# Building the Mixer's cosine and sine tables in one pass over split partitions

## The chip, the cores and the metric

The kernel runs on one core of a Trainium2 chip. It uses five engines, each with an instruction stream of its own that it executes in order: TensorE (PE: matmuls, and PEld: its weight loads), VectorE (DVE), ScalarE (ACT), GpSimd (POOL) and SyncE (SP, which here issues the DMA transfers). The metric is the device time of one execution in microseconds (us), as the median of several runs.

## The reference

One decoder layer with 1024 tokens of width 1024, in float32: a first SwiGLU feed-forward block, a mixer (half of its channels a short gated convolution, half an S5 state-space model, "SSM"), and a second feed-forward block. Each is modulated by `cond` (adaLN). What matters here:

```python
def reference(x, cond, ...):
    c_act = jax.nn.silu(cond)
    mod = c_act @ w_mod[l] + b_mod[l]        # shifts, scales and gates
    h = modulate(rms_norm(x, ffn1_norm[l]), sh1, sc1)
    x = x + 0.5 * g1 * swiglu(h, ffn1_w_gate[l], ffn1_w_up[l], ffn1_w_down[l])
    h = modulate(rms_norm(x, mix_norm[l]), sh2, sc2)
    b_gate, c_gate, v, u = jnp.split(h @ w_in[l], ...)
    y_conv = short_conv_mixer(b_gate, c_gate, v, conv_w[l])
    y_ssm = s5_mixer(u, lambda_re[l], lambda_im[l], log_dt[l], ...)
    ...                                       # norms, w_out, second feed-forward block

def s5_mixer(u, lambda_re, lambda_im, log_dt, b_re, b_im, c_re, c_im, ...):
    lam = lax.complex(lambda_re, lambda_im)
    dt = jnp.exp(log_dt)[:, None]
    lam_bar = jnp.exp(lam * dt)               # 32 groups x 64 states
    b_bar = ((lam_bar - 1) / lam)[..., None] * b
    bu = jnp.einsum('gpc,bsgc->bsgp', b_bar, uf)
    # state_t = lam_bar * state_(t-1) + bu_t, for all 1024 tokens
    _, states = lax.associative_scan(_ssm_combine, (a, bu), axis=1)
    y = jnp.einsum('gcp,bsgp->bsgc', c, states).real + d_skip * uf
    ...
```

The state-space model needs powers of `lam_bar`. The kernel keeps their phase as a rotation: for each group a table of cosines and one of sines over 128 steps.

## The kernel before

Every float32 product is made from high and low halves: `mm3` issues three matmuls of 128x512. The feed-forward blocks multiply by a seven-product scheme. `seven` makes one of the groups fa4 to fa10 of the first block in two sides, g and then u, each with seven left blocks of 4 `mm3`, that is 12 matmuls each. VectorE adds the products up out of PSUM banks. The seventh left block (S4) uses bank C again, so it waits until the side's third add has read that bank:

```python
SEVEN = (("A11", "A"), ("S1", "C"), ("S2", "B"), ("S3", "D"), ("A12", "A"), ("A22", "E"), ("S4", "C"))
...
elif n == 3:
    u3 = t2k(nm + "u3")
    add(u3, u2, "D")
    add(t1, u3, "C")      # the third add: fa5gt<-fa5gu,fa5gC in the trace
    out(1, 1, t1)
```

Tiles are named after the group and the side: `fa5gu`, `fa5gt` are partial sums of group fa5's gate side, `fa5gC` is its bank C, `fa5uu`, `fa5ut` are the same for the up side. At the end of a u side VectorE also makes some twenty operations that keep the result and its sums (`fa5A`, `fa5S`), stored to `kept...` for the down stages, where they come back as `fa1lA`, `fa1lS` and so on. The down stage of the first four groups, `down7("fad0")`, multiplies these by the weights `in_ds` and adds the products onto `x`. Every weight goes from a `raw` buffer through ScalarE (`CAST w<-raw`, the high half) and VectorE (`w<-raw,w`, the low half); GpSimd makes the sums of weight blocks (`sums`, lines 164, 165, 173 and 175 in `combine` and `split_done`).

Work that is not the feed-forward block's, the preparation of the Mixer above all, is put between the matmuls by a planner. `Clock` counts one tick for each `mm3`, and after every `period` ticks it takes one step of the side queue, that is, runs its generator up to the next `yield`. The period is 4 ticks in fa1 to fa3 and 7.75 in fa4 to fa10. The side queue holds `side1`: `ssm_base` (base tables for all groups), some combinations, and `ssm_batch(b)` for eight batches of four groups. `gate1` adds the steps of the modulation tiles (`wm`) while there are any. When group fa10 begins, what is left of the queue is run to its end, the side pools are closed, and `x` is loaded again into the space (`load_x`, first half at once, second half during `fad0`).

`ssm_batch` makes for each batch, with the names of the trace: `bb` and `cl`, `bl` (input and output coefficients, with `clt`, `blt` beside them), the rotors, and from two small TensorE products `kc` (with its diagonal `dg`) and `mi`. The tag `bt` has four buffers, which `cl`, `clt`, `bl`, `blt`, `rot`, `rott`, `kc`, `dg` and `mi` take in turn, so a tile waits until the one before in its buffer is read out. All results go to DRAM (`co_d`, `si_d`, `mk_d`, `mi_d`, `mo_d`) and come back in the Mixer stage. The rotors of before take two passes of 128 partitions: `rotors(0, subtract)` makes the cosines and `rotors(1, add)` the sines, with the second half of the partitions a repetition of the first, with the sine's sign turned there because `ro[1][hi]` has been negated. `st` are the step tables (`rs` in the trace), `bs` the base tables (`rt`).

Nearly all instructions are issued through the wrapper `InOrder`, whose `call` is line 107, so they carry L107 in the profile and are told apart by their tiles. The functions that the change touches:

Of the kernel before, what the change touches and what calls it, by code (L numbers as in the profile page):

```python
# [16 lines left out]
AF = mybir.ActivationFunctionType  # L17
ALU = mybir.AluOpType
# [213 lines left out]
def hymba_layer(ctx: ExitStack, tc, x_d, wm1_d, wmod_d, gu1_d, gs1_d, ds1_d, wl1_d, win_d, wout_d, glu_d, gu2_d, gs2_d, wd2_d, ds2_d, wl2_d, cols_d, cond_d, lam_d, bc_d, out_d):  # L232
    nc = tc.nc
    V, A, T, SP = (InOrder(tc, e) for e in (nc.vector, nc.scalar, nc.tensor, nc.sync))
# [30 lines left out]
    def sm(shape, name):  # L265
        return sm_ps.tile(shape, F32, tag="sm", name=name)
# [75 lines left out]
    def parts(name, where="A"):  # L342
        t = mov(name, where)
        return t[:, 0, :], t[:, 1, :]
# [427 lines left out]
    st = sm([P, 8], "p_st")  # L772
# [30 lines left out]
    for k in range(KT):  # L803
# [7 lines left out]
        for h in range(2):  # L811
            hi, lo = parts(f"h1{k}_{h}")
# [41 lines left out]
    co_d = scratch.tile([NB, P, GB * P], F32, name="co_d")  # L854
    si_d = scratch.tile([NB, P, GB * P], F32, name="si_d")
# [28 lines left out]
    def ssm_base(sb1):  # L884
# [4 lines left out]
        def s32(name):  # L889
            return sb1.tile([P, G], F32, tag=name, name=name)[:]  # L890
# [20 lines left out]
        dt, ar, th, r = s32("dt"), s32("ar"), s32("th"), s32("rr")  # L911
# [10 lines left out]
        ro = [s32("ro_r"), s32("ro_i")]  # L922
# [49 lines left out]
        lo, hi = slice(0, 64), slice(64, 128)  # L972
# [10 lines left out]
        V.tensor_tensor(out=w[0], in0=r, in1=r, op=ALU.mult)  # L983
        V.tensor_tensor(out=w[0], in0=w[0], in1=w[0], op=ALU.mult)
        V.tensor_tensor(out=r8[:], in0=w[0], in1=w[0], op=ALU.mult)
        V.tensor_scalar(out=ro[1][hi], in0=ro[1][hi], scalar1=-1.0, scalar2=None, op0=ALU.mult)
        cur = (ro[0], ro[1])
        base = [sb1.tile([P, 16, G], F32, tag=f"rb{i}", name=f"rb{i}") for i in range(2)]
        baset = [sb.tile([P, G, 16], F32, tag=f"rt{i}", name=f"rt{i}") for i in range(2)]
# [15 lines left out]
        for tab, cnt in ((base, 16), (step, 8)):  # L1005
# [3 lines left out]
            while n < cnt:  # L1009
# [4 lines left out]
                doubled(f"c{cnt}_{n}")  # L1014
                yield
                n *= 2
        for i in range(2):
            A.copy(baset[i][:], base[i][:].rearrange("p i g -> p g i"))
        yield
        zero = sb1.tile([CH, 112], F32, name="zero")  # L1020
        V.memset(zero[:], 0.0)
# [9 lines left out]
    def ssm_batch(b):  # L1031
# [9 lines left out]
        def bt(name):  # L1041
            return bp.tile([P, 576], F32, tag="bt", name=name, bufs=4)
# [20 lines left out]
        def v3(a):  # L1063
            return a[:, :512].rearrange("p (g m i) -> p g m i", g=GB, m=8)

        bs = [a[:, gs, :].unsqueeze(2).to_broadcast([P, GB, 8, 16]) for a in ssm["base"]]
        st = [a[:, :, gs].rearrange("p m g -> p g m").unsqueeze(3).to_broadcast([P, GB, 8, 16]) for a in ssm["step"]]

        def rotors(i, op):
            r, t = bt(f"rot{b}_{i}"), bt(f"rott{b}_{i}")  # L1070
            V.tensor_tensor(out=v3(r), in0=st[0], in1=bs[i], op=ALU.mult)
            V.tensor_tensor(out=v3(t), in0=st[1], in1=bs[1 - i], op=ALU.mult)
            yield
            V.tensor_tensor(out=r[:, :512], in0=r[:, :512], in1=t[:, :512], op=op)
            SP.dma_start((co_d, si_d)[i][b], r[:, :512])

        yield from rotors(0, ALU.subtract)
        yield

        kp = sm([CH, 512], f"kp{b}")  # L1080
# [5 lines left out]
        for g in range(GB):  # L1086
            T.transpose(tp[:, g * P : (g + 1) * P], bl[:, g * P : (g + 1) * P], ident[:])
        yield from gate1()
        yield from rotors(1, ALU.add)
        yield from gate1()  # L1090
        kc = bt(f"kc{b}")
        kc3 = kc[:CH, :512].rearrange("p (g m) -> p g m", g=GB)
# [4 lines left out]
            out=dg3,  # L1097
            in0=ident[:CH, :CH].unsqueeze(1).to_broadcast([CH, GB, CH]),
            in1=ssm["lam"][:CH, 3, gs].unsqueeze(2).to_broadcast([CH, GB, CH]),
            op=ALU.mult,  # L1100
# [11 lines left out]
    def gate1():  # L1112

        if fetched:
            mod_tile(mod_home if later[0][0] == G1 else None)
            yield
# [4 lines left out]
    def side1():  # L1121
        with tc.tile_pool(name="sb1", bufs=1, side="right") as sb1:
            yield from ssm_base(sb1)
        bps.append(side_open.enter_context(tc.tile_pool(name="bp", bufs=1, side="right")))
        mod_home.pool = side_open.enter_context(tc.tile_pool(name="wmp", bufs=1, side="right"))
        for _ in range(2):
            mod_fetch(mod_home)
        yield from combos(act1, "h1", "BBB")
        for b in range(NB):
            yield from ssm_batch(b)  # L1130
# [530 lines left out]
```

## Time and profile before

| quantity | value |
|---|---|
| runs | 1750.65, 1750.65 and 1752.18 us, median 1750.65 |
| profiled execution, its span | 1750.3 us |
| mean granted TensorE clock | 0.989 |
| VectorE instructions | 2286, busy 1300.6 us (74%) |
| ScalarE instructions | 934, busy 566.0 us (32%) |
| DMA moved | 304.54 MB, mean 174 GB/s |

The profile describes one execution. A row of a group gives line, engine, operation, output and inputs, shape and count, then busy time and mean duration in ns, then the engine's idle time ahead of these instructions and what ended it. Rows of the timeline give the start and the duration in us, and in brackets the idle time ahead with its releaser. Rows of the waits give what waited for what, us in total, times and longest. The row of a DMA issue gives SyncE's time for issuing; the landing is a separate row.

The span in 40 slices shows where VectorE is nearly full (each digit is the busy share of a slice in tenths):

```profile
PE   4999999999999999999999899989999999999996
DVE  7999999999855687744656977967777666676656
```

The tables of the Mixer are built in the first quarter, beside the groups fa1 to fa9; the down stage `fad0` lies at 480 to about 590 us.

### The profile page before, as it was taken

How to read it: one execution, taken by the hardware profiler on the slowest of the kernel's cores; microseconds unless marked ns; L12 is line 12 of the kernel's file. 1: busy time of each engine (PE TensorE's matmuls, PEld its weight loads, DVE VectorE, ACT ScalarE, POOL GpSimd, SP SyncE). 2: the span in 40 equal slices, each digit the busy share in tenths (PEclk: the TensorE clock that was granted, in tenths of full speed). 3: DMA queues.
4: the chain of work that ended last, by engine and by line, in shares of the span. 5: the costliest groups of instructions: out<-in, count | busy, mean ns of one | idle time of the engine just before them, and what ended most of it. 6: DMA issues, size and time to landing. Idle time of an engine off the chain costs nothing.

```text
span 1750.3 us, 20808 instructions
## 1 busy us (share of the span) xinstructions
PE 1677.9 (96%) x7532; PEld 1379.6 (79%) x7532; DVE 1300.6 (74%) x2286; ACT 566.0 (32%) x934; POOL 351.1 (20%) x241
## 2 busy tenths in 40 slices
PE   4999999999999999999999899989999999999996
PEld 3788887878787888887877778778888888888886
DVE  7999999999855687744656977967777666676656
ACT  4223234444322221332113424423343443322221
POOL 0000132222222221100000022023323322333211
PEclk9999999999999999999999999999999999999998
DMA  8245544444597877134654450113444334669312
GB/s 319 85 145 196 207 167 165 182 169 178 196 391 266 326 256 292 56 84 149 210 157 140 144 191 25 48 46 135 157 162 173 147 133 156 239 242 366 115 49 96
DMA packets 101080, 304.54 MB, mean 174 GB/s; under 512 B 19057, under 2 KB 34673, under 8 KB 89842
## 3 DMA queue, kind: packets, MB, share of 16 engines
q1 hardware_dynamic: 100978, 303.22, 48.4%
q8 instruction: 59, 0.97, 0.2%
q14 instruction: 43, 0.35, 0.1%
HBM read 212.47 MB, written 86.51 MB: 171 GB/s over the span
## 4 chain that ended last, share of the span: by engine, by line
PE 76%; DVE 14%; DMA 5%; issue 2%; POOL 1%; ACT 1%; SPq 1%; DVEq 0%; POOLq 0%; ACTq 0%
PE wo L107 4%; PE fald L107 3%; DVE w L107 3%; PE p L107 2%; PE fb10d L107 2%; PE fbd_0B L107 2%; PE fbd_1B L107 2%; PE u L107 2%; DMA swz<-si 2%; PE b L107 1%; DVE x L107 1%; PE c L107 1%; PE fa3u L107 1%; PE fb0g L107 1%; PE fa2g L107 1%
## 5 line engine op out<-in xcount | busy, mean ns | idle before, releaser
L107 ACT CAST w<-raw 128x512 fp32r<-128x512 f32 (+1 forms) x358 | 236.2, 689 | 484.3 <-issue 75.0
L107 DVE TENSOR_TENSOR w<-raw,w 128x512 fp32r<-128x512 f32 (+1 forms) x358 | 295.9, 845 | 107.3 <-ACT w L107 106.5
L164 POOL TENSOR_TENSOR sums<-raw 128x512 f32<-128x512 f32 x50 | 71.4, 1429 | 451.5 <-DMA raw<-in_gs 263.3
L173 POOL TENSOR_TENSOR raw<-sums,raw 128x512 f32<-128x512 f32 x50 | 77.7, 1554 | 371.1 <-DVE w L107 358.9
L175 POOL TENSOR_TENSOR raw<-raw 128x512 f32<-128x512 f32 x50 | 77.5, 1549 | 89.6 <-DVE w L107 73.0
L107 DVE CUSTOM_DVE_ANT_0 wm<-wm,cact 128x1024 f32<-128x1024 f32 x56 | 76.6, 1375 | 16.9 <-DMA wm<-in_wmod 16.9
L165 POOL TENSOR_TENSOR raw<-raw 128x512 f32<-128x512 f32 x50 | 77.3, 1547 | 3.2
L366 POOL TENSOR_TENSOR n3aq<-n3aq,n3aq 128x512 f32<-128x512 f32 x5 | 8.3, 1666 | 281.4 <-DMA wm<-in_wmod 255.7
L107 PE MATMUL p<-h,w 128*128 128x512 f32 x192 | 50.0, 423 | 8.0 <-DVE h L107 5.1
L107 DVE TENSOR_TENSOR w<-sums,w 128x512 fp32r<-128x512 f32 x50 | 52.5, 1063 | 3.6 <-ACT w L107 3.0
L107 PEld LDWEIGHTS p<-h,w 128*128 128x128 f32 x192 | 39.4, 207 | 18.4 <-DVE h L107 6.4
L107 PE MATMUL v<-h,w 128*128 128x512 f32 x192 | 46.9, 395 | 0.0
L107 PE MATMUL c<-h,w 128*128 128x512 f32 x192 | 46.6, 395 | 0.0
L107 PE MATMUL wo<-oa,w 128*128 128x512 f32 x192 | 45.6, 392 | 0.9 <-DVE w L107 0.7
L107 PE MATMUL b<-h,w 128*128 128x512 f32 x192 | 45.6, 394 | 0.0
L107 PE MATMUL wo<-ob,w 128*128 128x512 f32 x192 | 45.5, 392 | 0.0
L107 PE MATMUL u<-h,w 128*128 128x512 f32 x192 | 44.7, 392 | 0.2 <-DVE h L107 0.2
L107 PEld LDWEIGHTS wo<-oa,w 128*128 128x128 f32 x192 | 35.8, 188 | 9.0 <-DVE w L107 1.1
L107 PEld LDWEIGHTS u<-h,w 128*128 128x128 f32 x192 | 35.7, 188 | 8.2 <-DVE h L107 0.6
L107 PEld LDWEIGHTS wo<-ob,w 128*128 128x128 f32 x192 | 35.8, 188 | 7.7 <-DVE ob L107 0.4
L107 PEld LDWEIGHTS b<-h,w 128*128 128x128 f32 x192 | 35.6, 188 | 7.1
L107 PEld LDWEIGHTS c<-h,w 128*128 128x128 f32 x192 | 35.4, 188 | 7.0
(1565 smaller groups left out, 4056.2 us busy)
## 6 DMA issues: line engine op xcount, KB each, us to landing
raw<-in_gs SPq DMA_DIRECT2D x34, 1024.0 KB, 5.5
wm<-in_wmod SPq DMA_DIRECT2D x56, 512.0 KB, 5.3
raw<-in_ds SPq DMA_DIRECT2D x16, 1024.0 KB, 7.2
raw<-in_gu SPq DMA_DIRECT2D x10, 1024.0 KB, 7.0
mw<-in_wm SPq DMA_DIRECT2D x8, 1024.0 KB, 12.8
x<-in_x SPq DMA_DIRECT2D x16, 512.0 KB, 8.0
raw<-in_win SPq DMA_DIRECT2D x8, 1024.0 KB, 5.4
raw<-in_wl SPq DMA_DIRECT2D x5, 1024.0 KB, 6.7
```

What stands on the lines that cost most here:

```text
L107: r = getattr(self.engine, name)(*args, **kw)
L164: self.G.tensor_tensor(out=f, in0=r[2], in1=r[1], op=ALU.subtract)
L165: self.G.tensor_tensor(out=r[1], in0=r[1], in1=r[0], op=ALU.subtract)
L173: self.G.tensor_tensor(out=r, in0=s["t3"], in1=r, op=ALU.add)
L175: self.G.tensor_tensor(out=r, in0=self.chunk(j, 3), in1=r, op=ALU.subtract)
L366: nc.gpsimd.tensor_tensor(out=a, in0=a, in1=sq[:, :n], op=ALU.add)
```

## The change

The two passes become one. The cosines are made on partitions 0 to 63 and the sines on 64 to 127: the base tables `baset` are laid out for that, half by half, with the sign of one of them turned by ScalarE (so the negation of `ro[1][hi]` is dropped), and one product, one more product and one add on 128 partitions give both tables. ScalarE then negates the sines into `rott`'s upper half. Where before one store each filled `co_d[b]` and `si_d[b]`, four stores of 64 partitions now fill the two halves of each: the cosines twice, the sines, and the negated sines. The two tables in DRAM are the same as before. One `rotors` call less means three VectorE instructions less per batch (24 in all), one `yield` less per batch, eight more ScalarE instructions for the negations and two more for `baset`, and 32 instead of 16 stores.

```diff
-        V.tensor_scalar(out=ro[1][hi], in0=ro[1][hi], scalar1=-1.0, scalar2=None, op0=ALU.mult)
...
-        for i in range(2):
-            A.copy(baset[i][:], base[i][:].rearrange("p i g -> p g i"))
+        turned = [b[:].rearrange("p i g -> p g i") for b in base]
+        A.copy(baset[0][lo], turned[0][lo])
+        A.copy(baset[0][hi], turned[1][hi])
+        A.activation(baset[1][lo], turned[1][lo], AF.Copy, scale=-1.0)
+        A.copy(baset[1][hi], turned[0][hi])
         yield
...
-        def rotors(i, op):
-            r, t = bt(f"rot{b}_{i}"), bt(f"rott{b}_{i}")
-            V.tensor_tensor(out=v3(r), in0=st[0], in1=bs[i], op=ALU.mult)
-            V.tensor_tensor(out=v3(t), in0=st[1], in1=bs[1 - i], op=ALU.mult)
+        def rotors():
+
+            r, t = bt(f"rot{b}"), bt(f"rott{b}")
+            V.tensor_tensor(out=v3(r), in0=st[0], in1=bs[0], op=ALU.mult)
+            V.tensor_tensor(out=v3(t), in0=st[1], in1=bs[1], op=ALU.mult)
             yield
-            V.tensor_tensor(out=r[:, :512], in0=r[:, :512], in1=t[:, :512], op=op)
-            SP.dma_start((co_d, si_d)[i][b], r[:, :512])
-
-        yield from rotors(0, ALU.subtract)
+            V.tensor_tensor(out=r[:, :512], in0=r[:, :512], in1=t[:, :512], op=ALU.add)
+            A.activation(t[64:128, :512], r[64:128, :512], AF.Copy, scale=-1.0)
+            for half in (slice(0, 64), slice(64, 128)):
+                SP.dma_start(co_d[b, half], r[0:64, :512])
+            SP.dma_start(si_d[b, 0:64], r[64:128, :512])
+            SP.dma_start(si_d[b, 64:128], t[64:128, :512])
+
+        yield from rotors()
         yield
...
         yield from gate1()
-        yield from rotors(1, ALU.add)
         yield from gate1()
```

The order of the instructions on the engines is set by a scheduler, so other instructions move too. VectorE ahead of the third add of fa5's u side (`fa5ut<-fa5uu,fa5uC`), in the kernel before; `w` are halves of weights, `rot_0` and `rot_1` the first and second pass:

```order
640 L107 TENSOR_TENSOR rot_0_2891<-rs_989,rt_987 128x512
641 L107 TENSOR_TENSOR bl_2828<-bl_2828,blt_2829 128x512
642 L107 TENSOR_TENSOR rott_0_2892<-rs_990,rt_988 128x512
643 L107 TENSOR_TENSOR rot_0_2891<-rot_0_2891,rott_0_2892 128x512
644 L107 TENSOR_TENSOR fa5uu_2741<-fa5ut_2688,fa5uB 128x512
645 L107 TENSOR_TENSOR w_2746<-raw_2568,w_2746 128x512 x2
646 L107 TENSOR_TENSOR rot_1_2980<-rs_989,rt_988 128x512
647 L107 TENSOR_TENSOR rott_1_2981<-rs_990,rt_987 128x512
648 L107 TENSOR_TENSOR fa5uu_2782<-fa5uu_2741,fa5uD 128x512
649 L107 TENSOR_TENSOR rot_1_2980<-rot_1_2980,rott_1_2981 128x512
650 L107 TENSOR_TENSOR fa5ut_2688<-fa5uu_2782,fa5uC 128x512
```

The same place in the changed kernel:

```order
629 L107 TENSOR_TENSOR blt_2712<-tab_932,bb_2660 128x512
630 L107 TENSOR_TENSOR bl_2711<-bl_2711,blt_2712 128x512
631 L107 TENSOR_TENSOR rot_2747<-rs_988,rt_986 128x512
632 L107 TENSOR_TENSOR rott_2748<-rs_989,rt_987 128x512
633 L107 TENSOR_TENSOR rot_2747<-rot_2747,rott_2748 128x512
634 L107 TENSOR_TENSOR w_2726<-raw_2381,w_2726 128x512 x2
635 L107 TENSOR_TENSOR fa5uu_2764<-fa5ut_2724,fa5uB 128x512
636 L107 TENSOR_TENSOR w_2769<-raw_2584,w_2769 128x512 x2
637 L107 TENSOR_TENSOR fa5uu_2794<-fa5uu_2764,fa5uD 128x512
638 L107 TENSOR_TENSOR fa5ut_2724<-fa5uu_2794,fa5uC 128x512
```

Between the side's first add (`fa5uu` from bank B) and its third, three rotor instructions stood before, and none stands there now.

VectorE in the changed kernel, behind the rotors of the batch that falls into group fa6's g side; `dg` and `kc` take the buffers that `rott` and `rot` leave:

```order
681 L107 TENSOR_TENSOR rot_3019<-rs_988,rt_986 128x512
682 L107 TENSOR_TENSOR rott_3020<-rs_989,rt_987 128x512
683 L107 TENSOR_TENSOR rot_3019<-rot_3019,rott_3020 128x512
684 L107 TENSOR_TENSOR fa6gu_2999<-fa6gu_2999,fa6gE 128x512
685 L107 TENSOR_TENSOR w_3043<-sums_2954,w_3043 128x512
686 L107 TENSOR_TENSOR w_3043<-raw_2731,w_3043 128x512
687 L107 TENSOR_TENSOR fa6gu_2984<-fa6gu_2984,fa6gC 128x512
688 L107 TENSOR_TENSOR w_3083<-raw_2731,w_3083 128x512 x2
689 L107 TENSOR_TENSOR dg_3112<-ident,lam 16x64
690 L107 TENSOR_TENSOR bb_3163<-prm_3160,qr 128x64
691 L107 TENSOR_TENSOR kc_3110<-kc_3110,dg_3112 16x4x16
```

In the kernel before, `rot_1` of this batch (made in fa6's u side) has `dg` behind it only after the kept sums of fa6:

```order
704 L107 TENSOR_TENSOR rott_1_3289<-rs_990,rt_987 128x512
705 L107 TENSOR_TENSOR fa6ut_3054<-fa6uu_3136,fa6uC 128x512
706 L107 TENSOR_TENSOR rot_1_3288<-rot_1_3288,rott_1_3289 128x512
707 L107 TENSOR_TENSOR fa6ut_3054<-fa6ut_3054,fa6gt_2895 128x512
708 L107 TENSOR_TENSOR fa6gc_2987<-fa6gc_2987,fa6uA 128x512
...
727 L107 TENSOR_TENSOR w_3263<-raw_3061,w_3263 128x512
728 L107 TENSOR_TENSOR dg_3330<-ident,lam 16x64
```

`dg` has moved from 22 rows behind the last rotor add to 6 rows behind it.

SyncE ahead of the weights `in_ds` that the first down stage waits for, in the kernel before; `x` is the reload, 512 KB:

```order
268 L107 DMA fa3lS_4638<-kept3S_559 128x1024
269 L107 DMA fa4lS_4640<-kept4S_566 128x1024
270 L107 DMA x_1_4306<-in_x 128x1024
271 L107 DMA raw_4780<-in_ds 128x2048
272 L107 DMA raw_4812<-in_ds 128x2048
```

In the changed kernel the eight reloads stand together some forty rows earlier, ahead of the last `in_gs` load, and none is left in front of `in_ds`:

```order
238 L107 DMA x_1_4289<-in_x 128x1024
239 L107 DMA x_1_4291<-in_x 128x1024
240 L107 DMA raw_4152<-in_gs 128x2048
...
277 L107 DMA fa3lS_4623<-kept3S_559 128x1024
278 L107 DMA fa4lS_4625<-kept4S_566 128x1024
279 L107 DMA raw_4765<-in_ds 128x2048
280 L107 DMA raw_4797<-in_ds 128x2048
```

The loads have moved past the stores of fa9's and fa10's kept tiles, and the `in_ds` loads follow the `kept` loads directly.

## The prediction

> **What bounds the kernel now.** I read the busy shares first, then what TensorE waits for, and then the stages in which it waits.
>
> ```profile
> PE 1677.9 (96%) x7532; PEld 1379.6 (79%) x7532; DVE 1300.6 (74%) x2286; ACT 566.0 (32%) x934; POOL 351.1 (20%) x241
> ```
>
> TensorE is busy for 1677.9 of the profiled 1750.3 us, so this is a matmul kernel with small holes. The change adds no matmul and takes none away; it can only act through those holes. The waits of TensorE (what it waited for: us in total, times, longest) from 180 to 480 us, the stage in which the tables are built, and from 480 to 700:
>
> ```profile
> PE fa5uC L107 <- DVE fa5ut L107: 2.1, 1, 2.1
> PE fa7gC L107 <- DVE fa7gt L107: 2.6, 1, 2.6
> PE fa9gC L107 <- DVE fa9gt L107: 1.2, 1, 1.2
> ...
> PE fad_0A L107 <- DVE w L107: 2.8, 2, 1.7
> PE fad_0B L107 <- ACT w L107: 1.8, 1, 1.8
> ```
>
> The first three are one mechanism. The last left block of a side (S4) goes into bank C, which is free only when VectorE has made the side's third add (`fa?gt` or `fa?ut` from bank C). VectorE is late there, because the Mixer's tables stand in the same in-order queue. In the table by stretch (length, busy us and matmuls of PE, then PEld, DVE, ACT, POOL, clock, DMA share, GB/s) the price of each hole is seen by its missing matmuls:
>
> ```profile
> 290.00:310.00 20.00, 17.90 (x80) 14.52 (x79) 19.90 (x27) 6.78 (x12) 6.58 (x4) 1.00 0.39 159
> 350.00:370.00 20.00, 17.43 (x71) 13.90 (x70) 19.30 (x33) 8.72 (x17) 6.81 (x4) 0.91 0.53 183
> 430.00:450.00 20.00, 18.79 (x83) 15.25 (x82) 19.97 (x27) 7.66 (x14) 5.94 (x4) 1.00 0.59 212
> 530.00:550.00 20.00, 17.98 (x72) 14.11 (x71) 11.93 (x17) 2.56 (x5) 4.67 (x4) 0.92 0.96 369
> 550.00:570.00 20.00, 18.16 (x70) 13.95 (x69) 10.82 (x14) 5.14 (x10) 7.00 (x5) 0.91 0.53 189
> 570.00:590.00 20.00, 20.00 (x90) 16.58 (x89) 11.56 (x16) 2.90 (x5) 5.38 (x4) 1.00 0.88 348
> ```
>
> A full stretch holds 90 matmuls, 0.222 us each. The table stage misses 10, 19 and 7 of them: 2.2 + 4.2 + 1.6 = 8.0 us for 5.9 us of waits. The down stage `fad0` misses 18 and 20: 8.4 us. These 16.4 us are all that the change can win near its place. VectorE is nearly full in the first three stretches (19.3 to 19.97 of 20) and little over half full in the others.
>
> **The part on VectorE.** What the rotors take now (first three rows, 160 to 470 us, mean ns of one and idle time ahead), and what one takes undisturbed (min/median/max):
>
> ```profile
> L107 DVE TENSOR_TENSOR rot<-rot,rott 128x512 f32<-128x512 f32 x16 | 16.0, 1001 | 0.2
> L107 DVE TENSOR_TENSOR rott<-rs,rt 128x512 f32<-128x512 f32 x16 | 15.3, 959 | 2.1 <-DMA co_d<-rot 2.1
> L107 DVE TENSOR_TENSOR rot<-rs,rt 128x512 f32<-128x512 f32 x16 | 14.2, 885 | 0.1
> ...
> L107 DVE TENSOR_TENSOR rot<-rs,rt x16: 676/690/1784, 169.4 to 451.5; 128x512 f32<-128x512 f32 x16
> ```
>
> Together 45.5 us; half of them goes, 24 instructions and 22.7 us. At 0.60 us (the spacing of undisturbed neighbours, as 359.18 and 359.78 below) it is 14.4. The small negation of `ro[1]`, one instruction of under 0.4 us, goes too.
>
> That is not 22.7 us of the end, because the work is also pressed together. Each batch loses a `yield`: five steps instead of six once the modulation tiles are through. A step falls due every 7.75 ticks of three matmuls, 7.75 × 3 × 0.222 = 5.2 us. Eight batches so end about 41 us earlier, where now the last store of a table is issued at
>
> ```profile
> 463.15 0.53 SPq L107 DMA_DIRECT2D mi_d<-mi  x1
> ```
>
> The table work per batch, from the spacings in this piece of VectorE's timeline ahead of the dearest hole (start, duration), with TensorE's row last:
>
> ```profile
> 353.20 0.20 DVE L107 TENSOR_TENSOR dg<-ident,lam 16x64 f32<-16x64 f32 x1
> 353.42 0.69 DVE L107 TENSOR_TENSOR fa6S<-fa6uu,fa6S 128x512 fp32r<-128x512 f32 x1
> 354.03 1.32 DVE L107 TENSOR_TENSOR kc<-kc,dg 16x64 f32<-16x64 f32 x1
> 355.28 0.20 DVE L107 TENSOR_TENSOR bb<-prm,qr 128x64 f32<-128x64 f32 x1
> ...
> 358.50 0.76 DVE L107 TENSOR_TENSOR cl<-cl,clt 128x576 f32<-128x576 f32 x1
> 359.18 0.68 DVE L107 TENSOR_TENSOR fa7gu<-fa7gu,fa7gD 128x512 f32<-128x512 f32 x1
> 359.78 0.68 DVE L107 TENSOR_TENSOR w<-raw,w 128x512 fp32r<-128x512 f32 x1
> 360.38 0.68 DVE L107 TENSOR_TENSOR fa7gt<-fa7gu,fa7gC 128x512 f32<-128x512 f32 x1
> ...
> 361.21 4.24 PE L107 MATMUL fa7gC<-h1S,w 128*128 128x512 f32 x12 [2.57 <-DVE fa7gt L107]
> ```
>
> `dg` and `kc` take 0.2 + 1.25, `bb` and `cl` 3.9 less one add of the side among the rows left out (0.6), `bl` three times 0.60, the rotors six times 0.60: 10.2 us in six steps, 1.7 us a step. Afterwards 8.4 us in five steps, again 1.7. So the load per 5.2 us hardly changes; what ends is its duration. I counted what of it stands between two third adds in the two orders, at these spacings. From a u side to the next g side VectorE also makes the kept sums, and before, little fits: with 4.7, 4.7 and 5.3 us (fa6 to fa7, fa7 to fa8, fa8 to fa9) two of three boundaries made a hole, and so did the 9.5 us from fa5's g to its u. Afterwards the heavy ones are 5.3 us (fa5 to fa6), 4.7 (fa7 to fa8) and, from g to u, 7.1 (fa6) and 7.7 (fa7); behind fa8's u side there is none. Fitting the holes of before gives some 6.3 us of room from g to u, 2.3 from u to g, and a carried lead of at most 3.3. By that the new order waits 5.0 us instead of 5.9: the holes at fa5u and fa9g go, others come in fa6 to fa8. At 8.0 us lost for 5.9 waited, that is 6.8 lost, **1.2 won**.
>
> The dearest hole shows more than its wait: 2.57 us idle, but 19 matmuls (4.2 us) gone at a granted clock of 0.91, where the hole of 2.1 us lost 2.2 at 1.00. The Trainium skill ("TensorE: Matmul & The Clock Gate", "HAM oscillation — how this bites in real kernels") says that only idle gaps over about 3.4 us cost clock; by it the win would be 5.9 − 5.0 = 0.9. The trace disagrees at 2.57 us, so I keep 1.2.
>
> **ScalarE and the stores.** Eight negations of 64x512 are added, and the two turned copies of `rt` become four; the rows nearest to them, and the landing of the stores of before:
>
> ```profile
> L107 ACT COPY mi<-tp 128x512 f32<-128x512 f32 x8 | 4.6, 575 | 0.0
> L107 ACT COPY rt<-rb x2: 1147/1149/1151, 118.4 to 119.5; 128x512 f32<-128x512 f32 x2
> ...
> L107 SPq DMA_DIRECT2D co_d<-rot x8: 320/326/727, 177.6 to 449.8; - x8
> DMA to landing us min/median/max: 2.0/4.0/7.5
> ...
> L107 DVE TENSOR_TENSOR dg<-ident,lam 16x64 f32<-16x64 f32 x8 | 2.8, 344 | 1.9 <-DMA si_d<-rot 1.9
> ```
>
> A negation has the length of a row of `mi` on half the partitions: between 0.29 (half) and 0.58 us, I take 0.58, so 8 × 0.58 = 4.6 us of an engine that is 32% busy. The copies grow by at most 2 × 1.15 = 2.3 us, at 118 us, ahead of every wait listed. Nothing for the end. The stores go from 16 of 256 KB to 32 of 128 KB: SyncE issues 16 more, 16 × 0.33 = 5.3 us spread over 300, and the bytes stay. Their cost lies elsewhere: `kc` (filled by ScalarE) and `dg` (VectorE) take the buffers of `rot` and `rott` from a ring of four, and the last of four stores must have landed, `rott`'s behind a negation in ScalarE's queue. Already now this held VectorE once, for 1.9 us. In the new order `dg` stands 6 rows behind the rotor add in fa6, 3 in fa8, and 12 or more in five of eight batches. Queued behind `dg` are `kc`, `bb`, `cl` and the side's adds, for which TensorE waits. From both sides: nothing (landing 2.0, covered by rows of 0.6) to 8 × 3 us; I take **0.5 lost**, one wait like the one in the row that is only partly covered.
>
> **What moves behind the table stage.** The tables end sooner, so the pools close sooner and the eight reloads of `x` are issued together, ahead of the last `in_gs` load. Before, the last one stood directly ahead of the first `in_ds` loads that `fad0` waits for:
>
> ```profile
> 532.35 0.54 SPq L107 DMA_DIRECT2D x<-in_x  x1
> 532.98 1.28 SPq L107 DMA_DIRECT2D raw<-in_ds  x2
> ...
> 543.10 1.29 POOL L164 TENSOR_TENSOR sums<-raw 128x512 f32<-128x512 f32 x1 [34.72 <-DMA raw<-in_ds]
> ...
> 549.48 1.67 POOL L175 TENSOR_TENSOR raw<-raw 128x512 f32<-128x512 f32 x1 [1.45 <-DVE w L107]
> ...
> 546.66 0.57 PE L107 MATMUL fad_0A<-fa1lA,w 128*128 128x512 f32 x1 [1.71 <-DVE w L107]
> ...
> 556.58 1.52 PE L107 MATMUL fad_0B<-fa3lS,w 128*128 128x512 f32 x3 [1.81 <-ACT w L107]
> ```
>
> TensorE's two waits of 1.71 and 1.81 us hang on that landing at 543.1. Without the load in front, the issue comes 0.6 us sooner and 0.5 MB less lies ahead, 1.4 us at the 369 GB/s of that stretch: about 2 us. In GpSimd's order the second weight's sums now also pass L175 of the first, which had waited 1.45 us. So the first wait falls (with the clock it lost, 18 matmuls = 4.0 us), and the second shrinks. Bounds: 1.2 (the first shortened by the 0.6 us and a little clock) and 6.5 (nearly all of 8.4). I take **4.0 won**. The `in_gs` load now behind 4 MB of `x`, about 11 us at 369 GB/s, is a load ahead of need; I price it at 0, at most 2 if it comes late. The sum against the profiled execution: 1750.3 − 1.2 + 0.5 − 4.0 = 1745.6. The median of the runs, 1750.65, lies 0.35 above it: **1746.0**.
>
> **Rivals.**
> 1. *The holes all go.* VectorE loses 22.7 us in a stage where TensorE waits 5.9. For it: two of three known holes have rotors right ahead. Against it: 1.7 us a step as before. It gives 1750.65 − 8.0 − 4.0 = 1738.7.
> 2. *The holes only move.* As many waits in the new places, 8.0 us, and of `fad0` the lower bound, 1.2 won: 1749.5. For it: the equal density; the DMA share of 0.96 in 530 to 550, where one load less may change little.
> 3. *Slower: the stores hold the ring.* `dg` or `kc` waits for the last store in VectorE's in-order queue, and `kc` for the others in ScalarE's, ahead of casts. A store that is issued 2 us behind the rotor add (negation, four issues of 0.33) and takes the median 4.0 to land is done after 6; `dg` 3 or 6 rows behind the add arrives after 2 to 4. So two to four batches wait 2 to 4 us. It decides once that exceeds the lead of about 3 us at the u-to-g boundaries: four holes of 2.5 us, at the rate above 4 × 2.5 × 1.36 = 13.6 lost in all instead of 6.8, and a win of only 1.2 to 4.0 in `fad0`: 1750.65 + 5.6 − 1.2 = 1755.1, or 1752.3 with the 4.0. For it: the row of 1.9 us. Against it: the scheduler set most `dg` 12 rows off. The Trainium skill ("DMA: Bandwidth & Descriptors", "Rules for kernel authors") says that two transfers to disjoint partition halves serialize and that one over 128 partitions is to be preferred; by it the four half stores would land later than two whole ones, which is this rival's side; no row of before shows such a pair.
>
> **How the numbers follow.** The forecast has a chance of 0.48, rival 1 0.12, rival 2 0.20, rival 3 0.20. A measurement of this kernel tells about 0.2% (3.5 us) from no change, so faster is below 1747.2 and slower above 1754.2. The forecast's own spread (1743 to 1749) lies four fifths on the faster side, 0.38, and rival 1 adds 0.12: 0.50. Same: 0.10 of the forecast, nearly all of rival 2 (0.18) and the milder end of rival 3: 0.30. Slower: 0.20, most of rival 3 and a little for worse fitting orders. The range leaves out the full gain of rival 1 (half of it, 0.06) and the worse half of rival 3 (0.10): 1739 to 1755.
>
> **What would show it.** Right: VectorE's rotor groups with 8 instead of 16 each, near 23 us; the last `mi_d` store near 422 us instead of 463.15; no TensorE wait at fa5u or fa9g, but some in fa6 to fa8, 4 to 6 us in all; `raw<-in_ds` landing about 2 us sooner against `fad0`'s start, and its stretches with 80 or more matmuls. Wrong: idle of VectorE or ScalarE ahead of `dg`, `kc` released by `co_d` or `si_d` of 2 us and more (rival 3); no waits at all in 180 to 480 (rival 1); `fad0`'s waits unchanged (rival 2); or a wait for the `in_gs` load behind the `x` reloads.

## The result and the profile after

The changed kernel takes 1745.94 us (median of 9 runs, 1741.48 to 1749.23) against 1750.36 us for the kernel before (median of 9, 1747.36 to 1753.05): a ratio of 0.9974, 95% interval 0.9963 to 0.9985. A second set beside other kernels gave 0.9970 (0.9958 to 0.9982). The forecast was 1746.0, faster by over 0.2%. The total was met; of its two terms one was too small and the other had the wrong cause, as the experiments show.

The page of the changed kernel, busy shares:

```profile
PE 1672.0 (96%) x7532; PEld 1375.3 (79%) x7532; DVE 1291.1 (74%) x2261; ACT 573.3 (33%) x944; POOL 352.8 (20%) x241
```

The matmuls are the same 7532; VectorE has 25 instructions less. TensorE's waits, first in the table stage (180 to 480 us), then from 480 to 700:

```profile
PE fa6gC L107 <- DVE fa6gt L107: 0.9, 1, 0.9
PE fa4gC L107 <- DVE fa4gt L107: 0.2, 1, 0.2
...
PE fa8gC L107 <- DVE fa8gt L107: 2.2, 1, 2.2
PE fa7gC L107 <- DVE fa7gt L107: 0.3, 1, 0.3
...
PE fad_0A L107 <- DVE w L107: 3.9, 3, 1.9
PE fad_0A L107 <- ACT w L107: 0.3, 1, 0.3
```

The holes at fa5u and fa9g are gone, that at fa7g has shrunk from 2.6 to 0.3, and one of 2.2 has opened at fa8g: 3.6 us of waits instead of 5.9. In `fad0` the wait of `fad_0B` on ScalarE is gone. The same stretches as before, with the new hole's (busy us and matmuls per engine, clock, DMA share, GB/s):

```profile
350.00:370.00 20.00, 19.72 (x93) 15.71 (x92) 18.62 (x34) 10.05 (x19) 6.18 (x4) 1.00 0.63 214
390.00:410.00 20.00, 17.85 (x80) 14.45 (x78) 19.81 (x31) 6.58 (x12) 6.21 (x4) 1.00 0.52 178
530.00:550.00 20.00, 17.46 (x68) 13.34 (x67) 14.42 (x14) 4.05 (x8) 10.84 (x7) 0.91 0.77 312
550.00:570.00 20.00, 20.00 (x90) 16.55 (x89) 10.76 (x17) 4.91 (x9) 1.30 (x1) 1.00 0.72 257
```

`fad0` misses matmuls in one stretch of 20 us (22) where it missed them in two (18 and 20). These counts are good to a few only, since small products of the tables are counted too: 12 of the 93 in the first row. The rotors (160 to 470 us), and `dg`, which now takes a buffer that a store must leave:

```profile
L107 DVE TENSOR_TENSOR rot<-rot,rott 128x512 f32<-128x512 f32 x8 | 7.7, 960 | 0.1
L107 DVE TENSOR_TENSOR rot<-rs,rt 128x512 f32<-128x512 f32 x8 | 6.6, 823 | 0.0
L107 DVE TENSOR_TENSOR rott<-rs,rt 128x512 f32<-128x512 f32 x8 | 6.6, 823 | 0.0
...
L107 DVE TENSOR_TENSOR dg<-ident,lam 16x64 f32<-16x64 f32 x8 | 2.4, 296 | 0.7 <-DMA si_d<-rott 0.7
...
L107 ACT ACTIVATE rott<-rot 64x512 f32<-64x512 f32 x8 | 5.0, 629 | 21.6 <-DVE rot L107 15.6 <-issue 4.3 <-DMA wm<-in_wmod 1.7
```

Rotors: 20.9 us instead of 45.5, so 24.6 went (22.7 forecast). The eight negations cost ScalarE 5.0 (4.6 forecast).

To see where the time went I cut each profile at the first matmul of three tiles: `fa4gA` (the seven-product groups begin), `fad_0A` (the down stages) and `fald` (the last part of the first block). The starts stand behind the durations; first the kernel before, then the changed one:

```profile
L107 PE MATMUL fa4gA<-h,w x24: 388/390/390, 219.2 to 234.1; 128*128 128x512 f32 x24
L107 PE MATMUL fad_0A<-fa1lA,w x12: 389/390/567, 505.2 to 563.1; 128*128 128x512 f32 x12
L107 PE MATMUL fald<-fa0lA,w x96: 388/390/502, 667.8 to 722.9; 128*128 128x512 f32 x96
```

```profile
L107 PE MATMUL fa4gA<-h,w x24: 389/389/389, 220.2 to 233.6; 128*128 128x512 f32 x24
L107 PE MATMUL fad_0A<-fa1lA,w x12: 388/389/501, 500.9 to 555.3; 128*128 128x512 f32 x12
L107 PE MATMUL fald<-fa0lA,w x96: 389/389/389, 660.2 to 714.4; 128*128 128x512 f32 x96
```

Table stage: 505.2 − 219.2 = 286.0 before, 280.7 after. Down stages: 162.6 before, 159.3 after. All kernels, cut the same way (the stages are from one profile each; medians are from their own sets of runs, and each ratio is to the runs of the kernel before in the same set):

| kernel | table stage | down stages | median us | ratio to before (95%) |
|---|---|---|---|---|
| before | 286.0 | 162.6 | 1750.36 | |
| changed | 280.7 | 159.3 | 1745.94 | 0.9974 (0.9963 to 0.9985) |
| changed, again | 282.3 | 158.6 | 1745.33 | 0.9970 (0.9958 to 0.9982) |
| one pass, six steps | 280.8 | 162.4 | 1746.19 | 0.9962 (0.9947 to 0.9977) |
| two passes, five steps | 286.6 | 161.1 | 1752.54 | 1.0009 (1.0000 to 1.0017) |
| before, `x` early | 285.6 | 162.4 | 1748.88 | 0.9997 (0.9986 to 1.0007) |
| one pass, six steps, `x` early | 280.4 | 161.1 | 1744.57 | 0.9960 (0.9946 to 0.9974) |
| before, GpSimd's order | 286.2 | 159.6 | 1747.79 | 0.9988 (0.9975 to 1.0000) |
| changed, `x` late | 283.6 | 158.6 | 1744.35 | 0.9968 (0.9955 to 0.9980) |
| one pass, six steps, `x` early, GpSimd's order | 280.8 | 160.7 | 1742.80 | 0.9951 (0.9937 to 0.9965) |
| before, short sines | 287.9 | 161.8 | 1749.71 | 0.9995 (0.9985 to 1.0004) |
| before, short sines 2 | 282.7 | 161.8 | 1747.77 | 0.9987 (0.9976 to 0.9998) |
| before, one `rott` for both passes | 286.7 | 160.5 | 1751.16 | 1.0005 (0.9994 to 1.0015) |
| changed, `dg` outside the ring | 280.3 | 158.9 | 1744.34 | 0.9966 (0.9954 to 0.9978) |

### The profile page after: what moved, and what is told of

It is laid out like the page before. It is cut to its first block, busy times and chain, and to the rows that moved or that the text cites. A ratio compares the mean times of both kernels' runs of the same rounds, so it can differ in the third digit from the quotient of the medians.

```text
span 1739.7 us, 20839 instructions
## 1 busy us (share of the span) xinstructions
PE 1672.0 (96%) x7532; PEld 1375.3 (79%) x7532; DVE 1291.1 (74%) x2261; ACT 573.3 (33%) x944; POOL 352.8 (20%) x241
## 4 chain that ended last, share of the span: by engine, by line
PE 64%; DVE 8%; DMA 3%; issue 1%; ACT 0%; POOL 0%; SPq 0%; DVEq 0%; ACTq 0%; POOLq 0%
PE wo L107 4%; PE fald L107 3%; PE fb10d L107 2%; PE u L107 2%; PE fbd_1B L107 2%; PE fbd_0B L107 2%; PE fad_1B L107 2%; DVE w L107 2%; PE fad_0B L107 2%; PE b L107 2%; DMA swz<-si 1%; DVE x L107 1%; PE fb0g L107 1%; PE fbd_1C L107 1%; PE fbd_0C L107 1%; PE fbd_1A L107 1%
## 5 line engine op out<-in xcount | busy, mean ns | idle before, releaser
L107 DVE TENSOR_TENSOR w<-raw,w 128x512 fp32r<-128x512 f32 (+1 forms) x358 | 300.9, 860 | 100.8 <-ACT w L107 99.9
L164 POOL TENSOR_TENSOR sums<-raw 128x512 f32<-128x512 f32 x50 | 73.8, 1476 | 452.9 <-DMA raw<-in_gs 271.0
L175 POOL TENSOR_TENSOR raw<-raw 128x512 f32<-128x512 f32 x50 | 77.1, 1542 | 79.1 <-DVE w L107 79.1
L165 POOL TENSOR_TENSOR raw<-raw 128x512 f32<-128x512 f32 x50 | 77.3, 1547 | 3.1
L107 DVE TENSOR_TENSOR w<-sums,w 128x512 fp32r<-128x512 f32 x50 | 56.7, 1147 | 5.4 <-ACT w L107 4.8
L107 PE MATMUL wo<-ob,w 128*128 128x512 f32 x192 | 45.5, 392 | 0.0
```

Of the source, the lines that this page charges most:

```text
L107: r = getattr(self.engine, name)(*args, **kw)
L164: self.G.tensor_tensor(out=f, in0=r[2], in1=r[1], op=ALU.subtract)
L165: self.G.tensor_tensor(out=r[1], in0=r[1], in1=r[0], op=ALU.subtract)
L175: self.G.tensor_tensor(out=r, in0=self.chunk(j, 3), in1=r, op=ALU.subtract)
```

## The experiments: steps, work, and the reload of `x`

**One pass of rotors, but six steps a batch** (the dropped step is put back into the changed kernel):

```diff
         yield from gate1()
+        yield
         yield from gate1()
```

> The changed kernel with the dropped yield put back, so one pass of rotors in six steps a batch. In SyncE's order the last reload of x stands directly ahead of the in_ds loads again, as before the change. My theory (load per step decides the table stage, the place of the reload decides fad0): 8.4 us of table work in six steps is 1.4 us a step instead of 1.7, so TensorE's waits in the table stage fall to 0 to 1.5 us in all (8.0 us lost before, 1 now), and fad0 loses its 8.4 us as before: 1750.4 - 7 = 1743.4 us. Rival (the load per step does not matter, holes only move): 5 to 6 us of waits in the table stage and 1750 us.

Measured: 1746.19 us, table stage 280.8, down stages 162.4; waits of 1.2 (fa4g), 0.7 (fa7g) and 0.5 (fa9g). The one pass keeps its whole gain in the table stage with the old number of steps, and the down stages are as slow as before. The waits (2.4) lie above what my theory allowed and well below the rival's.

**Two passes, but five steps** (the second pass of the kernel before made at once):

```diff
-        yield from rotors(1, ALU.add)
+        for _ in rotors(1, ALU.add):
+            pass
```

> The kernel before with the second pass of rotors made in one step instead of two (its yield is skipped), so five steps a batch at the old work, 10.2 us in five steps, 2.0 us a step; the eight reloads of x stand together, early, as in the changed kernel. My theory: the table stage gets worse, 9 to 12 us of waits and 12 to 16 us lost instead of 8, and fad0 wins 4: 1750.4 + 6 - 4 = 1752 us (1749 to 1755). Rival (all of the gain comes from the earlier end of the tables, the work on VectorE does not matter): the time of the changed kernel, 1746 us, with waits of 4 us or less in the table stage.

Measured: 1752.54 us, near the 1752 expected, but not by that sum. The table stage loses only 0.6 more than before (286.6; waits of 7.1 us where 9 to 12 were expected), and the down stages win 1.5 where 4 were expected. The rival is out: fewer steps without less work bring nothing. So the load per step, on which my fit rested, explains little in either direction.

**The reloads of `x` early, nothing else:**

```diff
-            load_x(range(2), (0, 2))
+            load_x(range(2), (0, 2, 1, 3))
...
-    down7("fad0", lefts[0], 0, lambda left: fetch_chunk(1, left), lambda left: load_x(range(2), (1, 3)) if left == "A12" else None)
+    down7("fad0", lefts[0], 0, lambda left: fetch_chunk(1, left), None)
```

> The kernel before with all eight reloads of x issued in one place, so that none stands in front of the in_ds loads; rotors and steps as before. My theory: the waits at fa5u, fa7g and fa9g stay as they are, the in_ds loads land about 2 us sooner against fad0's last matmul, and fad0 wins 2 to 4 us: 1747.4 us (1746 to 1748.5). Rival (fad0's waits hang on GpSimd's and VectorE's work after the landing, not on the load in front): no change, 1750.4 us.

Measured: 0.9997, down stages 162.4 against 162.6. TensorE's waits from 495 to 600 us:

```profile
PE fad_0A L107 <- DVE w L107: 2.3, 1, 2.3
PE fad_0B L107 <- ACT w L107: 1.8, 1, 1.8
```

Both waits of `fad0` are there as before. The weights did come sooner: ScalarE's first cast of them begins 8.8 us after the issue (10.1 in the kernel before), and it then waited for VectorE's `fad_0u`, not for the load:

```profile
532.22 1.38 SPq L107 DMA_DIRECT2D raw<-in_ds  x2
541.01 0.62 ACT L107 CAST w<-raw 128x512 fp32r<-128x512 f32 x1 [13.12 <-DVE fad_0u L107]
```

So the step of the prediction that hung TensorE's two waits on this landing fell.

**One pass, six steps, and `x` early:**

> One pass of rotors in six steps a batch, and the eight reloads of x issued early. My theory adds the two gains: table stage 7 us, fad0 3 us, 1740.4 us (1738 to 1743), faster than both kernels. Rival (holes only move; fad0 does not hang on the reload): 1746 to 1750 us.

Measured: 1744.57 us, above the range that my theory gave (1738 to 1743). Table stage 280.4 as with six steps alone, down stages 161.1; the 1.8 us of `fad_0B` are there too.

## The experiments: what won in the down stages

The kernels with five steps have one thing more in common: at the second pair of `in_ds` weights GpSimd makes the second weight's sum (L164) ahead of the first weight's last one (L175). The order can be forced without a new instruction, by a scheduling dependence between two instructions of one engine:

```diff
...
                 t2 = self.G.tensor_tensor(out=r, in0=self.chunk(j, 3), in1=r, op=ALU.subtract)
+                if j == self.pair_early:
+                    info = mybir.DependencyInfo(mybir.DependencyClass.NoSync, mybir.DependencyReason.DATA)
+                    self.V.tc.add_manual_dep(t2.ins, self.first_sum[j + 1].ins.name, info, reason="order of issue")
```

> The kernel before with one thing moved: at the second pair of in_ds weights of fad0, GpSimd makes the second weight's sum (L164) ahead of the first weight's last sum (L175), as in the changed kernel's order; nothing else differs on any engine. New theory (fad0's gain came from this order, not from the reload of x): the 1.8 us wait of fad_0B on ScalarE's cast goes, the wait of fad_0A on VectorE stays near 1.9, fad0 to fald is 3 us shorter than the 162.6 of before, 1747.5 us. Rival (this place has no part in it; the gain in the changed kernel's profile is one execution's chance): 1750.4 us, with both waits or others of the same size.

Measured: 1747.79 us (0.9988, 0.9975 to 1.0000), down stages 159.6: 3.0 us less than before. TensorE's waits from 500 to 600 us:

```profile
PE fad_0A L107 <- DVE w L107: 2.5, 2, 2.0
PE fad_0B L107 <- ACT w L107: 0.5, 1, 0.5
```

Two rows changed places on one engine, and the second hole shrank from 1.8 to 0.5. TensorE's waits from 500 to 600 us fell by only 0.8 in all (3.8 to 3.0); most of the 3.0 is the clock that the second hole had cost. From 550 to 560 us, in the kernel before:

```profile
550.00:560.00 10.00, 8.16 (x27) 5.72 (x26) 6.03 (x7) 2.86 (x6) 7.00 (x5) 0.84 0.30 103
```

and in this one:

```profile
550.00:560.00 10.00, 9.05 (x38) 6.52 (x37) 6.44 (x7) 2.70 (x6) 5.72 (x4) 1.00 0.39 131
```

How it works is seen on GpSimd, first in this kernel, whose lines are numbered one higher (L165 and L176 are L164 and L175):

```profile
547.52 1.28 POOL L165 TENSOR_TENSOR sums<-raw 128x512 f32<-128x512 f32 x1
549.43 1.67 POOL L176 TENSOR_TENSOR raw<-raw 128x512 f32<-128x512 f32 x1 [0.63 <-DVE w L107]
```

In the kernel before, GpSimd stood 1.45 us for VectorE's `w` ahead of L175 (at 549.48) with the second sum behind it in its queue:

```profile
551.10 1.73 POOL L164 TENSOR_TENSOR sums<-raw 128x512 f32<-128x512 f32 x1
```

In the new order that sum fills the wait, and 0.63 is left of it.

**The changed kernel with the last reload of `x` held back**, so that it stands directly ahead of the `in_ds` loads again:

```diff
...
+            V.tensor_copy(out=xt[3][1][:, 0, 0:1], in_=x[1][0][:, 0:1])
             load_x([1], (3,))
```

> The changed kernel with the last reload of x held back until it stands directly ahead of the in_ds loads, as before the change (a copy of one column, on VectorE, holds it; the reload overwrites it). Step of the prediction (the reload in front costs 2 us of landing and so 2 to 4 us): 1748 to 1750 us, fad0 to fald near 162. New theory (the reload has no part in it): 1746 us, fad0 to fald 159 to 161 as in the changed kernel.

Measured: 1744.35 us, down stages 158.6. The reload in front costs nothing here either; this kernel has the changed kernel's order on GpSimd.

**The changed kernel again:**

> The changed kernel once more, for a second profile and beside the others on one chip. If the stages of the first profile are typical: 280.7 us from fa4g's first matmul to fad0's and 159.3 from there to fald's, at any time of the whole, and the rest of the spread of 8 us lies in the start and in the Mixer. If fad0's 159.3 was chance: 161 to 163. Time 1746 us.

Measured: 1745.33 us, stages of 282.3 and 158.6. The gain of the down stages is no chance. The table stage is 1.6 us longer than in the first profile, by one hole:

```profile
400.36 4.38 PE L107 MATMUL fa8gC<-h1S,w 128*128 128x512 f32 x12 [2.45 <-DVE fa8gt L107]
```

In the first profile the same place reads:

```profile
401.26 3.00 PE L107 MATMUL fa8gC<-h1S,w 128*128 128x512 f32 x12 [2.15 <-DVE fa8gt L107]
```

A hole 0.3 us longer makes the twelve matmuls behind it 1.4 us slower.

In `fad0` the two profiles of this one kernel differ the other way. The wait of 1.86 us at `fad_0A` (at 545.87) cost clock in the first one, as the 10 us around it show:

```profile
540.00:550.00 10.00, 7.80 (x25) 5.65 (x26) 8.01 (x7) 3.43 (x7) 7.92 (x5) 0.83 0.55 210
```

In the second profile the same wait, of 1.85 us, cost none:

```profile
540.00:550.00 10.00, 7.69 (x31) 5.20 (x30) 7.99 (x8) 3.02 (x6) 7.95 (x5) 1.00 0.63 240
...
546.34 0.50 PE L107 MATMUL fad_0A<-fa3lA,w 128*128 128x512 f32 x1 [1.85 <-DVE w L107]
```

**All that helped, together:**

> One pass of rotors in six steps, reloads of x early, and GpSimd's sums in the order of the changed kernel. New theory: the table stage as in the other one-pass kernels (280.4 us from fa4g to fad0), fad0 to fald 158 to 160, 1742.5 us, faster than both kernels. Rival (fad0 does not hang on GpSimd's order): 1744.5 us, as without it.

Measured: 1742.80 us, 0.9951 (0.9937 to 0.9965), the fastest median of all. `fad_0B` waits 0.5; the down stages are at 160.7, a little above the 158 to 160 expected and only 0.4 below the 161.1 of the same kernel without the order. There none of the waits of `fad0` cost clock (1.00 from 540 to 550 us); here the one of 2.1 at `fad_0A` did (0.83). Its interval and that of the changed kernel (0.9958 to 0.9982 in the same set) overlap, so it is faster than the kernel before; that it beats the changed one is likely and not shown.

**What the order is worth.** The 3.0 us of the forced order compare one profile with one, and whether a wait costs clock differs from profile to profile. With the old order `fad_0B` waits 1.8 us in all seven profiles, and their down stages take 160.5 to 162.6 us, 161.8 in the mean; with the new order (the changed kernel twice, its two variants, two passes in five steps and the two kernels with GpSimd's order) it waits 0.5 or nothing, and the seven take 158.6 to 161.1, 159.5 in the mean. That is 2.3 us, with the two groups overlapping. The fastest two of the old order (160.5 and 161.1) have the hole of 1.8 without a loss of clock, the slowest of the new one (161.1, two passes in five steps) lost clock at two other waits. The runs of the forced order, 0.12% faster with an interval that ends at 1.0000, agree with some 2 us; by themselves they do not rule out that it gained nothing.

## The experiments: what won in the table stage

**VectorE's time alone.** The kernel before, with the second pass cut to a sixteenth of its elements:

```diff
-            V.tensor_tensor(out=v3(r), in0=st[0], in1=bs[i], op=ALU.mult)
+            n = (16, 1)[i]
+            V.tensor_tensor(out=v3(r)[..., :n], in0=st[0][..., :n], in1=bs[i][..., :n], op=ALU.mult)
...
-            SP.dma_start((co_d, si_d)[i][b], r[:, :512])
+            firsts.append(r)
+            SP.dma_start((co_d, si_d)[i][b], firsts[0][:, :512])
```

> The kernel before, with the three VectorE instructions of each batch's second rotor pass cut from 128x512 to 128x32 (an element in 16); the sine table is not computed, its store sends the cosines instead, so that steps, stores and their sizes, the reloads of x and GpSimd's order stay as before. It leaves part of the output's work out. Theory (the time that VectorE saves is by itself the gain in the table stage): fa4g to fad0 281 us as with one pass in six steps, fad0 to fald 162 as before, 1746 us. Rival (the gain comes from the other order of the instructions or from the stores of halves): 285 to 286 us and 1750.

Measured: no gain, 1749.71 us as the rival had it, and a table stage of 287.9, longer than before. But the profile shows that the experiment brought a wait of its own. What VectorE waited for, from 160 to 480 us:

```profile
DVE rott L107 <- DMA si_d<-rot: 7.7, 5, 3.0
```

The cosine's buffer had to stay until both stores were through, and the next `rott` waited for it in VectorE's queue. So I sent a ready table instead, which holds nothing:

```diff
-            SP.dma_start((co_d, si_d)[i][b], firsts[0][:, :512])
+            SP.dma_start((co_d, si_d)[i][b], (r[:, :512], ssm["base"][0][:].rearrange("p g i -> p (g i)"))[i])
```

> As the first kernel with short sines (the second rotor pass of the kernel before cut to 128x32, sines not computed), but the sine store sends a ready table instead of the cosines, so that no buffer of the ring waits for it; these eight stores go early. Theory (VectorE's time and the stores' hold on the ring together set the holes): fa4g to fad0 280 to 282 us, as with one pass, fad0 to fald 162, 1746 us. Rival (neither matters, only the new order of instructions): 285 to 288 us, 1750.

Measured: 1747.77 us (0.9987, 0.9976 to 0.9998), table stage 282.7. Of the three holes only one is left, with VectorE's waits for a store below it:

```profile
PE fa7gC L107 <- DVE fa7gt L107: 3.2, 1, 3.2
...
DVE rott L107 <- DMA co_d<-rot: 5.6, 4, 2.6
```

Less time on VectorE, with the instructions' number and the steps unchanged, removes the holes at fa5u and fa9g and 3.3 us of the table stage (one profile; the runs gain 0.13%). The one pass brought 5.2 to 5.6 with the same steps. What it has besides is that no second `rott` waits for the first store: the kernel before shows VectorE idle for `co_d` and `si_d` for 2.1 (`rott`), 1.9 (`dg`) and 1.5 (`bb`, the row below), the changed kernel for 0.7.

```profile
DVE bb L107 <- DMA si_d<-rot: 1.5, 1, 1.5
```

That these waits make up the rest is argued, not shown. For it: ahead of the hole of 3.2 at fa7g in the last kernel VectorE stood 1.42 us for a store, and from there to the third add only 0.27 us more, so nothing behind this wait made up for it before TensorE's hole:

```profile
333.26 0.76 DVE L107 TENSOR_TENSOR rott<-rs,rt 128x32 f32<-128x32 f32 x1 [1.42 <-DMA co_d<-rot]
...
358.14 0.67 DVE L107 TENSOR_TENSOR fa7gt<-fa7gu,fa7gC 128x512 f32<-128x512 f32 x1
```

Against it: VectorE in the one pass with six steps waits 3.1 us for another store, and its table stage is 280.8 all the same:

```profile
DVE blt L107 <- DMA mk_d<-kc: 3.1, 1, 3.1
```

Between the two short kernels the table stage differs by 5.2 us; they differ in the sine store, in its time and in what it holds.

**The hold on the ring alone**, by letting both passes of the kernel before use one `rott`:

```diff
-            r, t = bt(f"rot{b}_{i}"), bt(f"rott{b}_{i}")
+            r = bt(f"rot{b}_{i}")
+            t = firsts[0] if firsts else bt(f"rott{b}_{i}")
+            firsts.append(t)
```

> The kernel before with both rotor passes at full work, but the second pass puts its product into the first pass's rott, so a batch takes one buffer less from the ring of four; all else stays. If the hold of the stores on the ring was a good part of the holes: VectorE's waits for co_d and si_d, 5.5 us before, fall below 2, fa4g to fad0 falls from 286 to 283 or 284, 1748 us. If VectorE's time alone counts: 286 and 1750.

Measured: 1.0005, table stage 286.7. It tells nothing, since the hold did not fall; it went from `rott` to `rot`:

```profile
DVE dg L107 <- DMA si_d<-rot: 2.9, 1, 2.9
...
DVE rot L107 <- DMA co_d<-rot: 2.1, 2, 1.2
DVE bb L107 <- DMA si_d<-rot: 1.7, 1, 1.7
```

**`dg` outside the ring in the changed kernel:**

```diff
-        dg = bt(f"dg{b}")
+        dg = bp.tile([P, GB * CH], F32, tag="dg", name=f"dg{b}", bufs=1)
```

> The changed kernel with dg in a buffer of its own, outside the ring of four, so that it waits for no store of rott, and kc follows in another slot. If the stores held the ring at a price (rival 3 of the prediction): the holes in fa6 to fa8 shrink, fa4g to fad0 falls by 2 us or more to 279 or less, 1743.5 us. My theory now (VectorE works without a pause ahead of the hole at fa8g, so the ring costs nothing there): 280.7 to 283.6 us as in three profiles of the changed kernel, and 1745 to 1746 us.

Measured: 1744.34 us, 280.3 and 158.9: VectorE's waits for stores are gone, and the time stays within that of the changed kernel. In the changed kernel the ring costs nothing that can be measured.

## Why the prediction was right, and where it was not

1. **The bound.** Right. The matmuls stayed, the gain came out of the holes on both sides, and the holes sit where VectorE's third add or the weights are late.
2. **VectorE's work and the tables' end.** 24.6 us went where 22.7 were forecast, and the last store of a table is issued at 419.1 us, forecast 422:

```profile
L107 SPq DMA_DIRECT2D mi_d<-mi x8: 326/528/1057, 196.5 to 419.1; - x8
```

3. **The term of the table stage: mis-sized.** 1.2 won less 0.5 lost was forecast. Cut by tiles the stage won 5.3, 3.7 and 2.4 in the three profiles that have the changed rotors and steps (280.7, 282.3 and, with `x` late, 283.6 against 286.0), 3.8 in the mean. The 286.0 is no chance: the two kernels that change nothing in the tables' work have 285.6 and 286.2. The step that failed is "the load per 5.2 us hardly changes", from which I concluded that the holes hardly change: two passes in five steps, 2.0 us a step, cost only 0.6 more, and one pass in six steps, 1.4, won 5.2, no more than the best profile of five. What counts is how far VectorE has fallen behind at each third add, and that follows from each piece ahead of it; how far the stores it waits for add to that is not shown. The places were right in part: holes at fa6g, fa7g and fa8g, none at fa5u and fa9g. Of the 5.9 us, 3.6 were left, where I had 5.0.
4. **The clock.** I charged the remaining waits with 8.0/5.9. In the first profile of the changed kernel no hole of the table stage cost clock; in the second the hole of 2.45 did. In `fad0` too the same wait cost clock in one profile and none in the other, so a fixed rate per us of waiting does not hold.
5. **The stores.** 0.5 lost: not seen. `dg` waited 0.7 in all, and taking it out of the ring changed nothing. I had counted only the waits that the change would add; it removed 5.5 and left 0.7 on VectorE, and 2.1 of the 5.5 stood in my own row of `rott`. One sign that I had named for rival 3 did come: ScalarE's `kc` waited for these stores, 3.4 us once (at 208.9, ahead of fa4g) and 1.0 once. No wait of TensorE follows from it; from 180 to 480 us it waits for VectorE alone.

```profile
ACT kc L107 <- DMA si_d<-rott: 3.4, 1, 3.4
...
ACT kc L107 <- DMA si_d<-rot: 1.0, 1, 1.0
```

6. **`fad0`: right size, wrong cause.** 4.0 forecast, 3.3 to 4.0 measured. I gave it chiefly to the reload of `x` in front of `in_ds`. Moved alone, the reload brings 0.2; put back into the changed kernel, it costs nothing. GpSimd's order, which I had named as a second reason, brings 3.0 alone in one profile and 2.3 over all. The step that failed is "TensorE's two waits of 1.71 and 1.81 us hang on that landing". The `in_ds` loads did come sooner, 8.7 us from issue to cast (10.1 before), but TensorE then waits for VectorE's halves and GpSimd's sums instead:

```profile
527.59 1.00 SPq L107 DMA_DIRECT2D raw<-in_ds  x2
...
536.27 0.62 ACT L107 CAST w<-raw 128x512 fp32r<-128x512 f32 x1 [11.77 <-DMA raw<-in_ds]
...
545.87 0.52 PE L107 MATMUL fad_0A<-fa3lA,w 128*128 128x512 f32 x1 [1.86 <-DVE w L107]
```

7. **The sum.** 4.7 was forecast; 4.4 was measured in the first set and 5.7 in the second (1750.99 and 1745.33). By the stages, with the means of those three profiles (282.2 and 158.8), it should be 3.8 + 3.8 = 7.6. The missing 2 to 3 us are not settled, and that the total was met is luck as far as the terms go: one term was too small, and the other's size rests on a cause that the prediction held for the lesser one. Part of it may lie ahead: the profiles with five steps reach `fa4gA` at 219.0 to 220.2, the other one-pass ones at 217.6 to 217.9. The rest is no larger than the spread of one stage which no experiment touches: from the Mixer's first product to the second block the fourteen profiles take 336.5 to 342.9 us. The first pair of profiles flatters the change, with 1750.3 and 1739.7 us of span: a run is some 1.8 us longer than its span (1741.48 for 1739.7), so the profiled execution of before was most likely the one of 1752.18, above its median, where I had set it 0.35 below.

The rivals: that all holes go (1738.7) did not come; that they only move is out, since 5.9 became 3.6; the slower one, the stores' hold on the ring, did not come. Of the two rules of the Trainium skill quoted in the prediction, the one against pairs of half transfers ("DMA: Bandwidth & Descriptors", "Rules for kernel authors") shows no loss here: the half stores of cosines and of sines landed after 2.6 us in the median, where the whole ones had taken 4.0 and 2.6. Their issue took SyncE 0.54 to 0.59 us each in the median, where I had put 0.33. The half stores of the cosines:

```profile
L107 SPq DMA_DIRECT2D co_d<-rot x16: 482/542/1141, 176.6 to 409.9; - x16
...
DMA to landing us min/median/max: 2.2/2.6/8.0
```

## What to carry to other kernels

A term of the sum needs its own experiment even where the total is met: here a term some three microseconds too small and an unexplained two to three in the other direction gave the right number. An engine in order that is full for hundreds of microseconds is not described by its load per step; list, for each deadline, what stands between it and the last one, with the stores that its buffers wait for. And when a small change wins far away from where it was made, compare the order on the helper engines row by row: two sums on GpSimd that changed places, and not the reload of `x` that stood out, moved the down stages by 2 to 3 us. And before one profile is held against another, look whether the same waits cost clock in both.

## What the hardware showed that I had not expected

What a wait of TensorE costs in clock does not follow from its length alone. In the table stage there seems to be an edge near 2.4 us. Holes of 2.07 to 2.35 us, five of them in these profiles, left the twelve matmuls behind them at 2.97 to 3.01 us; eight holes of 2.54 to 3.60 made them 4.24 to 5.46, and the 10 us window with them read a clock of 0.70 to 0.83. In between both occur: 2.45 cost 1.4 us, 2.49 nothing.

In the down stages shorter waits did it: of 24 waits of 1.70 to 2.33 us in the fourteen profiles, 16 left a clock of 0.57 to 0.68 in the 4 us behind them and eight left 1.00, the same place in the same kernel among both. So the Trainium skill's 3.4 us ("TensorE: Matmul & The Clock Gate", "HAM oscillation — how this bites in real kernels") is more than is needed here. What decides between two waits of one length these profiles do not show. One such hole makes most of the 1.6 us between the two table stages of the changed kernel, so it is one reason why the same kernel's times differ.
